# A decoder trunk's first norm with tokens on the partitions, and a first span of one row

## The chip, the cores and the metric

The kernel runs on one core of a Trainium2 chip. The metric is the time of one launch in device microseconds, lower is better. The profile was taken on one such execution.

## What is computed

Two decoder layers on 256 tokens of width 2048, all in float32: the first mixes tokens by retention with 8 heads, the second by a short gated convolution; each is followed by a SwiGLU block. Each of the four sub-layers begins with a norm whose scale and shift come from the conditioning vector c:

```
c_act = silu(c)
for i in range(DEPTH):
    mod = (c_act @ w_mod[i] + b_mod[i])[:, None, :]
    sh1, sc1, g1, sh2, sc2, g2 = split(mod, 6)
    h = rms_norm(x, norm1_g[i]) * (1 + sc1) + sh1
    x = x + g1 * mixer(h)          # layer 0: retention, layer 1: short convolution
    h = rms_norm(x, norm2_g[i]) * (1 + sc2) + sh2
    x = x + g2 * swiglu(h, ffn_w_in[i], ffn_w_out[i])
return rms_norm(x, final_g)
```

The retention starts with `h @ w_in`, which gives queries, keys, values and gates of all heads. Everything that the change touches lies before or in this product.

## The kernel before

**Layout.** Activations lie with the features on the partitions: 16 rows of 128 features by 256 tokens (`x[k]`, four tiles `x4`). A row of the normed activations, `h[k]`, is kept as a high part (float32r) and the remainder. Weights come as a stream of 1 MB chunks of 128 x 2048 (`w_all`), laid out on the host in the order of use. `prepare` takes half a chunk: ScalarE casts it to the high part (`hi`, L311), VectorE subtracts to get the low part (`lo`, L314). Each product is three passes on TensorE: high by high, high by low, low by high. There are four buffers for `hi` and four for `lo`, three for chunks. `take` keeps two halves ahead of TensorE after the first span.

**The modulation** is a product with a vector. It is not done on TensorE: each tile of `w_mod` (1 MB, features of one row by 2048) is multiplied by the spread `silu(c)` (`cb`) and summed by one instruction of VectorE (`reduced`, L657). Row k of the first norm needs two such tiles, `SC1` and `SH1`. `column` makes the two columns of the row on ScalarE (L666), `row` applies them (u at L682, h's high part at L685 on ScalarE, its low part at L686 on VectorE). `loaded` fetches the tiles into four buffers; `ahead_of(k)` fetches those of row k.

**Spans.** `ret_in` can't begin with all rows, as they are made one after the other. So the first product is cut into spans: a span is two heads' queries, keys and gates, over some rows, in eight banks of PSUM. `SPANS` lists them: heads 0, 1 over rows 0 and 1; heads 2, 3 over rows 0 to 5; heads 0, 1 over rows 2 to 9; heads 2, 3 over rows 6 to 11; head 4 over all 16 rows, four banks. For one row of two heads TensorE takes one chunk. After a span, `held` puts its banks away: the first time by a copy on ScalarE (L644), later by an add on VectorE (L641). The first four adds come at once, the next four are put into the list `due`.

**Order.** TensorE's order is that of the program. In this start VectorE's and ScalarE's order is written out by hand too (`manual_schedule`). In the first span each row's reductions stand between its two heads (`both_reduced`). In the spans behind it, `due` holds pairs of a step and something to do (make row k, reduce a tile for the next row, put a bank away), and `more`, which is called at each half step, does what is due. A step is one row of two heads.

**The first norm.** x is loaded in four pieces, ScalarE squares it, VectorE adds the squares, four small matmuls with ones sum over the partitions (`norm_sums`, L434), ScalarE makes the mean, GpSimd takes the root (L760), four matmuls spread it over the partitions (`norm_spread`, L455), ScalarE copies it out. VectorE then multiplies two rows of x by it at a time (`norm_two`, L674). Meanwhile TensorE spreads c over the partitions (L725), and ScalarE applies silu to it (L729).

All loads are issued by SyncE's queue in the order of the program; an issue waits there until its buffer is free.

Of the kernel before, what the change touches and what calls it, by code (L numbers as in the profile page):

```python
# [10 lines left out]
F32 = mybir.dt.float32  # L11
# [6 lines left out]
P = 128  # L18
# [169 lines left out]
def trunk(ctx: ExitStack, tc: tile.TileContext, x_in, c_in, pos_in, w_mod, cols_in, gain_in, tab_in, w_all, out):  # L188
# [46 lines left out]
    def mod_raw(t, pool=wpool, bufs=RAW_BUFS):  # L235
        raw = pool.tile([P, CHUNK], F32, tag="raw", name=name("raw"), bufs=bufs)
        nc.sync.dma_start(raw, w_mod[t])
        return raw
# [51 lines left out]
    def fetch():  # L290
        raw = wpool.tile([P, CHUNK], F32, tag="raw", name=name("raw"), bufs=RAW_BUFS)
        nc.sync.dma_start(raw, w_all[n_fetched[0]])
        n_fetched[0] += 1
        fetched.append(raw)
# [39 lines left out]
    def bank():  # L334
        return ps.tile([P, 2, S], F32, tag="bank", name=name("bank"))
# [245 lines left out]
    with ExitStack() as inner:  # L581
# [64 lines left out]
        with tc.tile_pool(name="start", bufs=1) as sp:  # L646
            raws_of, totals = {}, {}

            def loaded(which, k):
                if k < KT:  # L650
                    raws_of[which, k] = mod_raw(which * KT + k, sp, START_RAWS)

            def reduced(which, k):
                if k < KT:
                    raw = raws_of.pop((which, k))
                    total = totals[which, k] = tmp("msum", (P, 1), bufs=4)
                    nc.vector.scalar_tensor_tensor(raw, raw, 1.0, cb, op0=ALU.mult, op1=ALU.mult, accum_out=total)  # L657
# [11 lines left out]
            normed_x = {}  # L669

            def norm_two(i):
                t = normed_x[i] = rm.tile([P, 2, S], F32, tag=f"mid{18 + i % 2}", name=name("two"))
                both = x4[i // 2][:, 2 * (i % 2) : 2 * (i % 2) + 2, :]
                nc.vector.tensor_tensor(t, both, rb.unsqueeze(1).to_broadcast([P, 2, S]), op=ALU.mult)  # L674

            def row(k):

                a, b = (column(SC1, k), column(SH1, k)) if k else first_cols
                t = normed_x[k // 2][:, k % 2, :]
                full = tmp("u", bufs=3)  # L680
                if k:
                    nc.scalar.activation(full, t, AF.Identity, bias=b, scale=a)  # L682
                else:
                    nc.vector.tensor_scalar(full, t, a, b, op0=ALU.mult, op1=ALU.add)
                nc.scalar.activation(h[k][:, 0, :], t, AF.Identity, bias=b, scale=a)  # L685
                return lambda: nc.vector.tensor_tensor(  # L686
                    h[k][:, 1, :], full, h[k][:, 0, :].bitcast(F32), op=ALU.subtract
                )
# [6 lines left out]
            def after_scale(k):  # L695
                reduced(SH1, k + 1)
                if k % 2 == 0 and k + 2 < KT:
                    norm_two(k // 2 + 1)

            def ahead_of(k):  # L700
                loaded(SC1, k)
                loaded(SH1, k)
                if k < FIRST_KS + 2:
                    fetch()

            with tc.manual_schedule(engines={mybir.EngineType.DVE, mybir.EngineType.Activation}):
                c_row = sp.tile([1, D], F32, tag="raw", name=name("raw"), bufs=START_RAWS)
                nc.sync.dma_start(c_row, c_in)
                for i in range(4):
                    nc.sync.dma_start(x4[i], x_in[:, 4 * i : 4 * i + 4, :])  # L710
                loaded(SC1, 0)
                nc.sync.dma_start(cols, cols_in)
                loaded(SH1, 0)
                nc.sync.dma_start(tab, tab_in[:, : 1 + P])
                fetch()
# [3 lines left out]
                nc.vector.memset(eps, EPS)  # L719
                ahead_of(1)  # L720
# [10 lines left out]
                def square(i):  # L731

                    sq = [rm.tile([P, 2, S], F32, tag=f"mid{2 * i + n}", name=name("sq")) for n in range(2)]
                    for n in range(2):
                        nc.scalar.activation(sq[n], x4[i][:, 2 * n : 2 * n + 2, :], AF.Square)
                    return sq

                def added(a, b):
                    for n in range(2):
                        nc.vector.tensor_tensor(a[n], a[n], b[n], op=ALU.add)  # L740

                acc = square(0)
                for i in range(1, 4):
                    added(acc, square(i))
                for i in range(4):
                    silu(i)
                nc.vector.tensor_tensor(acc[0], acc[0], acc[1], op=ALU.add)
                nc.vector.tensor_tensor(acc[0][:, 0, :], acc[0][:, 0, :], acc[0][:, 1, :], op=ALU.add)
                pt = norm_sums([acc[0][:, 0, :]])
                reduced(SC1, 0)  # L750
                gain_1 = const.tile([P, KT], F32, tag="gain1", name="gain1")
                nc.vector.scalar_tensor_tensor(
                    gain_1, b_mod[:, SC1 * KT : (SC1 + 1) * KT], 1.0, gain[0][0], op0=ALU.add, op1=ALU.mult
                )
                reduced(SH1, 0)
                mean = tmp("rs", (P, 2), bufs=4)
                nc.scalar.activation(mean, pt[:, 0, 0:2], AF.Identity, bias=eps, scale=1.0 / D)
                first_cols = [column(SC1, 0)]
                r = tmp("rs", (P, 2), bufs=4)
                nc.gpsimd.tensor_tensor(r, mean, half, op=ALU.pow)  # L760
                rb = tmp("rb", bufs=1)
                nc.scalar.copy(rb, norm_spread(r))
                norm_two(0)
# [16 lines left out]
            at = 0.0  # L780
            for k in range(FIRST_KS, KT):
                steps = ROW_STEPS[k >= SPANS[1][1][1]]
                due.append((at, lambda k=k: (row(k)(), ahead_of(k + 2))))
                due.append((at + steps / 3, lambda k=k: reduced(SC1, k + 1)))
                due.append((at + steps * 2 / 3, lambda k=k: after_scale(k)))
                at += steps
            for i, turn in enumerate(angles()):
                due.append((at + (i + 1) * 0.5, turn))
# [13 lines left out]
            with tc.manual_schedule(engines={mybir.EngineType.DVE, mybir.EngineType.Activation}):  # L802
# [10 lines left out]
                while due:  # L813
                    due.pop(0)[1]()

# [341 lines left out]
```

## Time and profile before

| | |
|---|---|
| median of 3 runs | 2620.13 us (2616.75 to 2620.81) |
| the profiled execution | 2621.43 us, its span 2619.7 us |
| TensorE busy | 2587.4 us, 99% of the span |
| VectorE busy | 1982.7 us, 76% |
| ScalarE busy | 1248.5 us, 48% |
| moved by DMA | 689.62 MB, mean 263 GB/s |

The span counts from the first to the last instruction of the profiled execution; the device time includes what lies around it. In the profile's views PE is TensorE's matmuls, PEld its weight loads, DVE is VectorE, ACT ScalarE, POOL GpSimd, SPq SyncE's queue of DMA issues. A row of the timeline gives start and length in us, engine, line, operation, what is written and read, the number of merged instructions, and in brackets how long the engine had been idle and what released it.

### The profile page before, as it was taken

The numbers are of one execution on the slowest core, as the hardware profiler recorded it, in microseconds if no ns is written. First come the engines' busy times: TensorE is split into PE (matmuls) and PEld (weight loads), VectorE is DVE, ScalarE is ACT, GpSimd is POOL, SyncE is SP. The second block draws the span as 40 slices with busy tenths as digits, with TensorE's granted clock in tenths as the row PEclk, the third lists the DMA queues.
The fourth block names the chain that finished last, engine by engine and source line by source line (L and its number), as shares of the span: only waits on it lengthen the run. The fifth ranks groups of instructions, "written<-read, shape, count | busy, mean of one in ns | idle before, by whom it ended". The sixth has DMA issues, their size and how long they took to land.

```text
span 2619.7 us, 37456 instructions
## 1 busy us (share of the span) xinstructions
PE 2587.4 (99%) x14867; PEld 2283.7 (87%) x14867; DVE 1982.7 (76%) x2490; ACT 1248.5 (48%) x1784; POOL 148.4 (6%) x232
## 2 busy tenths in 40 slices
PE   7999999999999999999999999999999999999998
PEld 6898889888899888888888898888998888888887
DVE  7988977887698887777777889888887765555554
ACT  5544543444456444344444454444564443444443
POOL 0000000110000001101100001100000000000000
PEclk9999999999999999999999999999999999999999
DMA  9976668877686887777777758777777775555554
GB/s 398 393 288 224 252 243 305 291 253 277 243 303 244 314 298 275 286 282 283 283 277 273 282 216 326 293 267 265 265 268 261 263 251 193 193 187 186 191 193 145
DMA packets 96834, 689.62 MB, mean 263 GB/s; under 512 B 10753, under 2 KB 12177, under 8 KB 13713
## 3 DMA queue, kind: packets, MB, share of 16 engines
q1 hardware_dynamic: 96658, 687.23, 71.1%
q8 instruction: 116, 1.90, 0.3%
q14 instruction: 60, 0.49, 0.0%
HBM read 685.08 MB, written 2.11 MB: 262 GB/s over the span
## 4 chain that ended last, share of the span: by engine, by line
PE 87%; DMA 6%; DVE 5%; issue 1%; ACT 1%; ACTq 0%; POOLq 0%; POOL 0%; DVEq 0%
PE bank L356 37%; PE bank L359 19%; PE bank L372 7%; PE bank L371 7%; PE bank L373 7%; DMA raw<-w_all 4%; DVE lo L314 2%; PE bank L398 2%; PE bank L397 2%; PE bank L396 2%; DMA raw<-w_mod 2%; PE bank L529 1%; PE bank L531 1%; PE bank L530 1%; DVE raw L657 1%
## 5 line engine op out<-in xcount | busy, mean ns | idle before, releaser
L314 DVE TENSOR_TENSOR lo<-raw,hi 128x1024 fp32r<-128x1024 f32 x912 | 1113.0, 1224 | 562.3 <-ACT hi L311 560.5
L311 ACT CAST hi<-raw 128x1024 fp32r<-128x1024 f32 x912 | 953.6, 1050 | 1084.1 <-PE bank L356 478.9
L356 PE MATMUL bank<-h,hi 128*128 128x512 f32 x3296 | 1144.2, 390 | 0.2 <-ACT hi L311 0.2
L359 PE MATMUL bank<-h,lo 128*128 128x256 f32 x3296 | 929.6, 282 | 1.3 <-DVE lo L314 1.3
L356 PEld LDWEIGHTS bank<-h,hi 128*128 128x128 f32 x3296 | 618.6, 188 | 129.7 <-ACT hi L311 0.5
L359 PEld LDWEIGHTS bank<-h,lo 128*128 128x128 f32 x3296 | 622.9, 189 | 2.0 <-DVE lo L314 1.9
L245 DVE SCALAR_TENSOR_TENSOR raw<-raw,cb 128x2048 f32<-128x2048 f32 x160 | 365.8, 2286 | 24.6 <-DMA raw<-w_mod 24.2
L356 PE MATMUL bank<-mid,hi 128*128 128x512 f32 x922 | 319.8, 390 | 0.0
L359 PE MATMUL bank<-mid,lo 128*128 128x256 f32 x922 | 260.1, 282 | 1.4 <-DVE lo L314 1.4
L356 PEld LDWEIGHTS bank<-mid,hi 128*128 128x128 f32 x922 | 173.1, 188 | 36.2
L371 PE MATMUL bank<-hi,h 128*128 128x512 f32 x512 | 201.4, 393 | 2.0 <-DVE rm L641 1.4
L372 PE MATMUL bank<-lo,h 128*128 128x512 f32 x512 | 200.1, 391 | 0.8 <-DVE lo L314 0.8
L373 PE MATMUL bank<-hi,h 128*128 128x512 f32 x512 | 199.4, 389 | 0.0
L359 PEld LDWEIGHTS bank<-mid,lo 128*128 128x128 f32 x922 | 174.3, 189 | 1.7 <-DVE lo L314 1.7
L356 PE MATMUL bank<-rm,hi 128*128 128x512 f32 x496 | 172.5, 390 | 0.0
L398 PE MATMUL bank<-h,lo 128*128 128x256 f32 x512 | 146.2, 285 | 5.4 <-DVE lo L314 5.4
L396 PE MATMUL bank<-h,hi 128*128 128x256 f32 x512 | 145.6, 284 | 3.3 <-ACT h L685 3.3
L397 PE MATMUL bank<-h,hi 128*128 128x256 f32 x512 | 145.5, 284 | 0.7 <-DVE h L686 0.7
L359 PE MATMUL bank<-rm,lo 128*128 128x256 f32 x496 | 139.8, 282 | 0.0
L371 PE MATMUL bank<-hi,mid 128*128 128x512 f32 x352 | 137.0, 389 | 0.0
L372 PE MATMUL bank<-lo,mid 128*128 128x512 f32 x352 | 136.9, 389 | 0.0
L373 PE MATMUL bank<-hi,mid 128*128 128x512 f32 x352 | 136.9, 389 | 0.0
(175 smaller groups left out, 2700.0 us busy)
## 6 DMA issues: line engine op xcount, KB each, us to landing
raw<-w_all SPq DMA_DIRECT2D x456, 1024.0 KB, 4.8
raw<-w_mod SPq DMA_DIRECT2D x192, 1024.0 KB, 5.1
x<-x_in SPq DMA_DIRECT2D x4, 512.0 KB, 5.5
out<-xt SPq DMA_DIRECT2D x4, 512.0 KB, 3.0
decay<-tab_in SPq DMA_DIRECT2D x8, 128.0 KB, 2.4
x<-gain_in SPq DMA_DIRECT2D x2, 512.0 KB, 6.8
x<-gate_row SPq DMA_DIRECT2D x2, 512.0 KB, 5.3
cols<-cols_in SPq DMA_DIRECT2D x1, 152.0 KB, 8.6
```

What stands on the lines that cost most here:

```text
L245: nc.vector.scalar_tensor_tensor(raw, raw, 1.0, cb, op0=ALU.mult, op1=ALU.mult, accum_out=total)
L311: nc.scalar.copy(hi, raw)
L314: nc.vector.tensor_tensor(lo, raw, hi.bitcast(F32), op=ALU.subtract)
L356: nc.tensor.matmul(pt, hi, h, start=fresh and k == g.ks[0], stop=False, skip_group_check=True)
L359: nc.tensor.matmul(pt[:, 1, :], lo, h[:, 0, :], start=False, stop=last and k == g.ks[-1], skip_group_check=True)
L371: nc.tensor.matmul(o, ht[:, 0, :], hi, start=first, stop=False)
L372: nc.tensor.matmul(o, ht[:, 0, :], lo, start=False, stop=False)
L373: nc.tensor.matmul(o, ht[:, 1, :], hi, start=False, stop=last)
L396: nc.tensor.matmul(pt, hi, h[:, 0, :], start=first, stop=False, skip_group_check=True)
L397: nc.tensor.matmul(pt, hi, h[:, 1, :], start=False, stop=False, skip_group_check=True)
L398: nc.tensor.matmul(pt, lo, h[:, 0, :], start=False, stop=last, skip_group_check=True)
L529: nc.tensor.matmul(pt, hi, high, start=k == 0, stop=False, skip_group_check=True)
```

## The change

Nothing is changed behind the spans. In the start:

- x comes a second way, `xt_in`: tokens on the partitions, two halves of 128 tokens by 2048, in eight pieces of 128 x 512. The sums of squares run along the free dimension, half of the pieces on ScalarE and half on VectorE, each in one instruction with its sum.
- The roots are put on a diagonal (ScalarE scales the identity by them), and 32 matmuls turn x to the layout with features on the partitions and multiply it by the roots at once. ScalarE copies the eight banks into `x4` (`kept`), three of them before row 0 and five behind it. `x4` holds the normed x during the spans; the plain x is loaded into it after the last span.
- The first span has one row instead of two, and there are six spans in place of five. The reductions of row 1 come behind the first span and behind the preparation of chunk 1.
- The steps at which rows, loads and reductions are due are set anew, and the angles of the rotary embedding come later.
- The first loads are cut in two parts, and so are the first two reductions.

```diff
-SPANS = (((0, 1), (0, 2)), ((2, 3), (0, 6)), ((0, 1), (2, 10)), ((2, 3), (6, 12)), ((4,), (0, 16)))
+SPANS = (
+    ((0, 1), (0, 1)), ((2, 3), (0, 2)), ((0, 1), (1, 6)), ((2, 3), (2, 10)), ((0, 1), (6, 12)), ((4,), (0, 16)),
+)
-ROW_STEPS = (1.4, 2.0)
-START_RAWS = 4
+ROWS_AT, ROW_STEPS = (0.0, 2.4, 3.6, 4.8, 5.9), 2.0
+LOADS_AT, ANGLE_STEPS = (0.4, 1.9, 2.9), 6
+START_RAWS, KEPT_FIRST = 4, 3
...
             def row(k):
...
-                t = normed_x[k // 2][:, k % 2, :]
+                t = x[k]
...
             def both_reduced(k):
                 reduced(SC1, k + 1)
-                after_scale(k)
+                reduced(SH1, k + 1)
                 ahead_of(k + 2)
...
-                for i in range(4):
-                    nc.sync.dma_start(x4[i], x_in[:, 4 * i : 4 * i + 4, :])
-                loaded(SC1, 0)
+                for t, i in pieces:
+                    xt[t, i] = rm.tile([P, DV], F32, tag=f"mid{4 * t + i}", name=name("xt"))
+                    nc.sync.dma_start(xt[t, i], xt_in[t, :, i * DV : (i + 1) * DV])
+                nc.sync.dma_start(tab, tab_in[:, : 1 + P])
+                loaded(SC1, 0, 2)
                 nc.sync.dma_start(cols, cols_in)
-                loaded(SH1, 0)
-                nc.sync.dma_start(tab, tab_in[:, : 1 + P])
-                fetch()
+                loaded(SH1, 0, 2)
+                fetch(2)
...
+                warm = tmp("rs", (P, 2), bufs=4)
+                nc.gpsimd.tensor_tensor(warm, ones[:, 0:2], half, op=ALU.pow)
+                fetch()
                 ahead_of(1)
...
+                def squares_of(t, i):
+                    v, total = xt[t, i], part[:, i, t : t + 1]
+                    if i % 2:
+                        nc.vector.scalar_tensor_tensor(
+                            left[1], v, 1.0, v, op0=ALU.mult, op1=ALU.mult, accum_out=total
+                        )
+                    else:
+                        nc.scalar.activation(left[0], v, AF.Square, accum_out=total)
+                for t, i in pieces:
+                    squares_of(t, i)
+                    if i % 2:
+                        silu(2 * t + i // 2)
...
+                for t in range(2):
+                    nc.scalar.activation(roots[:, t, :], ident, AF.Identity, scale=r[:, t : t + 1])
+                for i in range(KT // 2):
+                    pt = bank()
                     for n in range(2):
+                        for t in range(2):
+                            j, c = divmod(2 * i + n, 4)
+                            v = xt[t, j][:, c * P : (c + 1) * P]
+                            nc.tensor.matmul(
+                                pt[:, n, t * P : (t + 1) * P], v, roots[:, t, :], start=True, stop=True
+                            )
+                    turned.append(pt)
+                def kept(i):
+                    nc.scalar.copy(x4[i // 2][:, 2 * (i % 2) : 2 * (i % 2) + 2, :], turned[i])
...
                     low[0]()
-                pts = packed(RET_SPANS[0], h, before=before, between=both_reduced, banks=banks)
+                    for i in range(KEPT_FIRST, KT // 2) if not k else ():
+                        kept(i)
+                pts = packed(RET_SPANS[0], h, before=before, banks=banks)
                 prepare()
                 prepare()
+                both_reduced(0)
...
+            for i, at in enumerate(rows_made):
+                k = FIRST_KS + i
+                due.append((at, lambda k=k: row(k)()))
+                due.append((LOADS_AT[i] if i < len(LOADS_AT) else at, lambda k=k: ahead_of(k + 2)))
+                if i:
+                    gap = min((at - rows_made[i - 1]) / 3, 0.5)
+                    due.append((at - 2 * gap, lambda k=k: reduced(SC1, k)))
+                    due.append((at - gap, lambda k=k: reduced(SH1, k)))
...
+        for i in range(4):
+            nc.sync.dma_start(x4[i], x_in[:, 4 * i : 4 * i + 4, :])
```

More of the change, by code (lines that the diff above doesn't have):

```diff
@@ L742, in trunk @@
[L742 to L750, printed above, removed]
+                part = rm.tile([P, 4, 2], F32, tag="mid8", name=name("part"))
@@ new lines, in trunk @@
+                for t, i in pieces:
+                    squares_of(t, i)
+                    if i % 2:
+                        silu(2 * t + i // 2)
+                both = tmp("rs", (P, 2), bufs=4)
+                nc.vector.tensor_tensor(part[:, 0:2, :], part[:, 0:2, :], part[:, 2:4, :], op=ALU.add)
+                nc.vector.tensor_tensor(both, part[:, 0, :], part[:, 1, :], op=ALU.add)
+                mean = tmp("rs", (P, 2), bufs=4)
+                nc.scalar.activation(mean, both, AF.Identity, bias=eps, scale=1.0 / D)
@@ L754, in trunk @@
                 )
-                reduced(SH1, 0)
-                mean = tmp("rs", (P, 2), bufs=4)
-                nc.scalar.activation(mean, pt[:, 0, 0:2], AF.Identity, bias=eps, scale=1.0 / D)
+                reduced(SH1, 0, 2)
+                kept(0)
                 first_cols = [column(SC1, 0)]
[L759 to L763, printed above, removed]
+                for i in range(1, KEPT_FIRST):
+                    kept(i)
                 first_cols.append(column(SH1, 0))
@@ L779, in trunk @@
             due, step = [], [0.0]
[L780 to L788, printed above, removed]
+            rows_made = list(ROWS_AT)
+            while len(rows_made) < KT - FIRST_KS:
+                rows_made.append(rows_made[-1] + ROW_STEPS)
+            for i, at in enumerate(rows_made):
[6 more added lines that the diff above has]
+                    due.append((at - gap, lambda k=k: reduced(SH1, k)))
+            due.sort(key=lambda d: d[0])
+            at = rows_made[-1] + ROW_STEPS
+            turns = []
+            due.append((rows_made[-4], lambda: turns.extend(angles())))
+            for i in range(ANGLE_STEPS):
+                due.append((at + (i + 1) * 0.5, lambda i=i: turns[i]()))
+            due.sort(key=lambda d: d[0])
             def more(n):
@@ L1150 @@
             tc,
-            *[aps[k] for k in ("x_in", "c_in", "pos_in", "w_mod", "cols_in", "gain_in", "tab_in", "w_all")],
+            *[aps[k] for k in ("x_in", "xt_in", "c_in", "pos_in", "w_mod", "cols_in", "gain_in", "tab_in", "w_all")],
             out,
```

59 lines of the change are left out of this document (31 added, 28 removed).

## The prediction

> **What bounds the kernel now.** The page first, then the busy time by stage.
>
> ```profile
> span 2619.7 us, 37456 instructions
> PE 2587.4 (99%) x14867; PEld 2283.7 (87%) x14867; DVE 1982.7 (76%) x2490; ACT 1248.5 (48%) x1784; POOL 148.4 (6%) x232
> 10.00:60.00 50.00, 37.92 (x217) 33.07 (x218) 43.01 (x47) 27.87 (x49) 1.39 (x1) 1.00 1.01 419
> 60.00:130.00 70.00, 66.69 (x418) 59.27 (x417) 67.59 (x70) 39.86 (x60) 0.00 (x0) 1.00 0.97 395
> 130.00:200.00 70.00, 70.00 (x448) 63.55 (x447) 59.78 (x71) 33.98 (x45) 0.00 (x0) 1.00 0.73 279
> ```
>
> The last three rows are stretches of the start (window, length, busy us of PE, PEld, DVE, ACT, POOL, clock, DMA share, GB/s). From 130 us on TensorE has no gap here; it misses 32.3 us in the whole span, 15.4 of them in the first two of these stretches, where the DMA engines are full (1.01) and VectorE is busy 67.6 of 70 us. The change only touches this start. Whatever it moves in the time at which TensorE has done the spans, it moves in the end. So I count not busy time but starts of TensorE's half steps (one row of one head, one half chunk of weights).
>
> ```profile
> 2.61 7.16 PE L725 MATMUL bank<-raw,ones 1*128 1x512 f32 x8 [2.61 <-DMA raw<-c_in]
> 15.47 1.22 PE L455 MATMUL bank<-tab,rs 128*128 128x128 f32 x4 [1.82 <-POOL rs L760]
> 19.18 0.58 PE L396 MATMUL bank<-h,hi 128*128 128x256 f32 x1 [2.48 <-ACT h L685]
> 22.57 0.41 PE L398 MATMUL bank<-h,lo 128*128 128x256 f32 x1
> 22.78 0.57 PE L371 MATMUL bank<-hi,h 128*128 128x512 f32 x1
> 68.38 0.39 PE L396 MATMUL bank<-h,hi 128*128 128x256 f32 x1 [0.84 <-ACT h L685]
> 71.80 0.28 PE L396 MATMUL bank<-h,hi 128*128 128x256 f32 x1
> 85.90 0.28 PE L396 MATMUL bank<-h,hi 128*128 128x256 f32 x1
> 89.77 0.28 PE L396 MATMUL bank<-h,hi 128*128 128x256 f32 x1
> 120.79 0.28 PE L396 MATMUL bank<-h,hi 128*128 128x256 f32 x1
> 122.22 0.40 PE L371 MATMUL bank<-hi,h 128*128 128x512 f32 x1
> 122.92 0.40 PE L371 MATMUL bank<-hi,h 128*128 128x512 f32 x1
> 123.61 0.28 PE L396 MATMUL bank<-h,hi 128*128 128x256 f32 x1
> 125.89 0.50 PE L371 MATMUL bank<-hi,h 128*128 128x512 f32 x1 [0.69 <-DVE rm L641]
> 127.62 0.50 PE L371 MATMUL bank<-hi,h 128*128 128x512 f32 x1 [0.76 <-DVE rm L641]
> 128.42 0.28 PE L396 MATMUL bank<-h,hi 128*128 128x256 f32 x1
> 1886.21 0.60 PE L455 MATMUL bank<-tab,rs 128*128 128x128 f32 x4
> ```
>
> An undisturbed half is 120.79 to 123.61, 2.82 us; a step of two heads is 5.64. The first starts at 19.18. Row 5 (eighth step) starts at 68.38: seven steps are 39.5, so 9.7 us are lost by then. After it, the halves from 68.38, 85.90 and 123.61 are late by 0.60, 1.05 and 1.99: 3.64. The last is a change of spans: the new span's eighth bank waits until VectorE has added the old one to what is held (L641).
>
> VectorE's queue, then ScalarE's with GpSimd's root:
>
> ```profile
> 55.36 2.29 DVE L657 SCALAR_TENSOR_TENSOR raw<-raw,cb 128x2048 f32<-128x2048 f32 x1
> 57.57 1.22 DVE L314 TENSOR_TENSOR lo<-raw,hi 128x1024 fp32r<-128x1024 f32 x1
> 59.15 0.43 DVE L686 TENSOR_TENSOR h<-u,h 128x256 fp32r<-128x256 f32 x1 [0.36 <-ACT h L685]
> 60.09 1.23 DVE L314 TENSOR_TENSOR lo<-raw,hi 128x1024 fp32r<-128x1024 f32 x1 [0.51 <-ACT hi L311]
> 61.23 2.28 DVE L657 SCALAR_TENSOR_TENSOR raw<-raw,cb 128x2048 f32<-128x2048 f32 x1
> 63.44 1.22 DVE L314 TENSOR_TENSOR lo<-raw,hi 128x1024 fp32r<-128x1024 f32 x1
> 117.88 2.47 DVE L641 TENSOR_TENSOR rm<-rm,bank 128x512 f32<-128x512 f32 x4
> 126.88 0.69 DVE L641 TENSOR_TENSOR rm<-rm,bank 128x512 f32<-128x512 f32 x1
> 10.49 2.04 ACT L729 ACTIVATE cb<-bank 128x512 f32<-128x512 f32 x4
> 13.69 0.26 ACT L757 ACTIVATE rs<-bank,eps 128x2 f32<-128x2 f32 x1 [1.15 <-PE bank L434]
> 16.73 0.37 ACT L762 COPY rb<-bank 128x256 f32<-128x256 f32 x1 [1.35 <-PE bank L455]
> 25.04 1.04 ACT L311 CAST hi<-raw 128x1024 fp32r<-128x1024 f32 x1 [4.98 <-DMA raw<-w_all]
> 35.84 3.98 ACT L644 COPY rm<-bank 128x512 f32<-128x512 f32 x8
> 40.58 2.00 ACT L311 CAST hi<-raw 128x1024 fp32r<-128x1024 f32 x2 [0.76 <-DMA raw<-w_all]
> 57.69 0.30 ACT L666 ACTIVATE s<-msum,cols 128x1 f32<-128x1 f32 x1 [2.96 <-DVE raw L657]
> 58.02 0.60 ACT L682 ACTIVATE u<-two,s,a 128x256 f32<-128x256 f32 x1
> 58.53 0.59 ACT L685 ACTIVATE h<-two,s,a 128x256 fp32r<-128x256 f32 x1
> 14.03 1.39 POOL L760 TENSOR_TENSOR rs<-rs,half 128x2 f32<-128x2 f32 x1 [13.60 <-ACT rs L757]
> ```
>
> Start to start: a reduction 2.21 (61.23 to 63.44), a lo 1.14 (60.09 to 61.23), a row's low half 0.34 of its 0.43, an add 0.60, a hi cast 0.95 to 1.0, a PSUM copy on ScalarE 0.50. A row needs its shift column after the reduction (55.36 to 57.69), then u and h: h is ready 3.8 us after the reduction started. If one lo lies between, VectorE idles 0.43 before the low half, if none, 1.6; after it, 0.6 until the next hi.
>
> Chunk 1 and chunk 3, with 8.2 and 14.2 MB queued up to their ends, were waited for until 25.04 and 40.58: 2.59 us per MB. I use this as the landing clock; the change keeps the queue full.
>
> **The change, part by part.**
>
> *Start.* The squares leave the chain (two adds of small tiles remain), and so do 4+4 small matmuls. c's spread still ends at 2.61+7.16 = 9.8; the last silu (2.04/4), the mean 0.26, the root 1.39 and one diagonal (at most the 0.37 of L762) give 12.4. New: 32 f32 matmuls with 128 columns, two instructions each like L455's, 64 in all, ahead of row 0 in TensorE's queue. Slow, L455's four start (1.22-0.58)/3 = 0.21 apart; fast, (0.60-0.27)/3 = 0.11. Bounds: 7.0 to 13.7 us. From 19.18 the array turned fast at 22.78, after 3.6 us. So 17 slow ones, then 47 × 0.11: they end at 21.2. The first matmul of row 0 comes 2 us later than the 19.18 of before, but fast. [...]
>
> *Copies.* ScalarE's copies of the turned banks are 0.50 each, eight, in place of eight squares. Three precede row 0: the third bank is turned at about 17.1 (24 instructions), copy and shift column end at 17.9, chunk 0's first half (4.7 MB) has landed at 16.0, its hi and h[0] are ready at 19.5, its lo and the low half at 20.5, hidden since TensorE turns until 21.2. Five stand ahead of hi 0b: the last waits for the end of the turning, 21.5, so hi 0b starts at 22.0 and VectorE's lo 0b at 23.1. VectorE idles for it; row 1's reductions, which could run there, now stand behind the lo of chunk 1.
>
> *VectorE from 23.1 to row 5*, in the order that `due` gives (0b is chunk 0, second half; S and H the scale's and shift's reductions):
> 0b 1a 1b S1 H1 = 7.8, to 30.9 (S1 and H1 have landed at 22.4 and 25.0); idle 1.6, row 1, idle 0.6: 33.4. 2a 2b 3a S2 3b H2 4a = 10.1: 43.6; 0.43, row 2, 0.6: 45.0. 4b S3 5a H3 5b = 7.8: 52.8; 0.43, row 3: 53.6. S4 6a H4 6b = 6.7: 60.3; 0.43, row 4: 61.1. Chunk 7 has 22.2 MB up to its end: 61.3, its hi a cast later, so 7a starts at 62.4 (chunk 5, at 45.8, and chunk 6, at 53.5, are in time). 7a S5 7b H5 = 6.7: 69.1; 1.6: row 5 at 70.7.
> TensorE meets row 1 at step 2 about 2 us late, rows 3, 4 and 5 again late; row 5 starts at 70.7 against 68.38: **+2.3**. The half products (norm_two, 0.6 for two rows) are gone, but H5 now directly precedes row 5, and chunk 7 lands no earlier. A start up to 0.7 earlier is eaten by chunk 7.
>
> *Changes of spans.* Two in place of one put eight banks against VectorE's adds (the two first ones go to ScalarE's copies, 35.84, in time; the last needs four banks). In before, adds from 117.88 to 127.57 made the bank, wanted at 120.79+2.82+1.43+0.70 = 125.7, 1.9 late. By the new `due` S6 lies behind the fourth add and H6 before the seventh. From row 5: low half and 8a 8b to 73.9, four adds 76.3, S6 2.2, add, 9a, add, H6, add, 9b, add: 85.4. Wanted: step end 76.5 + 4.95 = 81.45; **3.95** late. At the next change VectorE has slack, but its adds can start only after lo 16b, whose buffer TensorE frees one step before the end E: lo done at E-3.4, four adds E-1.0, then the same 9.1 and a 0.1 to TensorE: E+8.2 against E+4.95: **3.25**.
>
> *Hidden.* The second load of x, 2 MB at about 195 us, meets a share of 0.73 and no waiting copy (5 us at the landing clock if it had to be waited for whole). The angles' later place puts some 6 us of VectorE behind the last span's weights, two prepared halves (5.6) cover it: 0 to 2. GpSimd's warm-up root lies ahead of xt: 0. xt's eight loads move the same 2 MB.
>
> Sum: 2.3 + 3.95 + 3.25 - 3.64 (the losses that followed in before) = **+5.9**. The profiled execution took 2621.43 (its span and 1.7 around it), 1.3 above the median of 2620.13; on the median: 2626.0.
>
> **The rivals.**
>
> *The turning stays slow.* [...] 64 × 0.21 ends at 26.1 and lo 0b starts at 28.0, 4.9 later; chunk 7's wait of 1.3 is swallowed, so row 5 is 3.6 later: +9.5, 2629.6. Chance 0.18. [...]
>
> *VectorE gets ahead* (faster). One mechanism: the reductions of rows 1 to 5 are done while TensorE still multiplies reused rows, so that each h is ready when it is wanted. Then only the start (21.2 for 19.18), row 1's 2 us and two changes of spans at the old 1.99 remain: 21.2 + 2 + 4 = 27.2, against 19.18 + 9.7 + 3.64 = 32.5 now: -5.3, 2614.8. It decides if row 5 starts by 64. For it: the landing clock allows it up to chunk 7 (61.3 and two casts). Against it: 15 lo, 10 reductions and 5 low halves are 41 us of VectorE's work from 23.1 on, and TensorE needs 39.5 us for its seven steps from 21.2 on. Chance 0.14.
>
> **How the numbers follow.** The forecast has 0.68. Its own range is +2.5 to +9: row 5 within 2 us (chunk 7 and the idle bubbles), each change of spans within 1, the angles 0 to 2. 0.2%, 5.2 us, is about what a measurement of this kernel can tell from no change; 55 in 100 of the forecast's range lie above it. Slower: 0.18 + 0.37 = 0.55; within: 0.31; faster: 0.14. The 8 in 10 reach from 2614 to 2633; what is left out is the better half of the faster rival and the far end of the slow turning.
>
> **What would show it.** Right: 64 matmuls on the diagonal from about 12.4 to 21, lo 0b near 23, no idle VectorE over 1.7 us from there to row 5, TensorE waiting for h at rows 3 to 5, row 5 at 70 to 72, and two waits for L641's adds of 3 to 4 us. Wrong: row 5 before 66, or changes of spans without a wait; then the sum turns.

## The result and the profile after

| | before | after |
|---|---|---|
| median of 7 runs each, taken together | 2617.21 us (2616.25 to 2620.81) | 2626.78 us (2624.60 to 2627.70) |
| ratio after to before | | 1.0032, 95% interval 1.0020 to 1.0044 |
| profiled execution, its span | 2621.43, 2619.7 | 2626.78, 2625.0 |

The change makes the kernel slower by 0.32%, some 8 us by the ratio, 9.6 by the medians. The absolute time lies 0.8 from the predicted one, but that flatters the forecast: it added 5.9 to a base of 2620.1, the median of three runs, and all seven taken together put the base at 2617.2. The difference is what has to be explained: 5.9 forecast, in a range of 2.5 to 9, and 8 to 10 found.

The page of after, its first lines, and the stretches of the start as in the prediction (window, length, busy us of PE, PEld, DVE, ACT, POOL, clock, DMA share, GB/s):

```profile
span 2625.0 us, 37613 instructions
PE 2596.1 (99%) x14923; PEld 2293.8 (87%) x14923; DVE 1983.3 (76%) x2498; ACT 1253.1 (48%) x1793; POOL 144.2 (5%) x233
10.00:60.00 50.00, 42.54 (x260) 38.56 (x261) 39.37 (x50) 34.76 (x60) 1.61 (x1) 0.97 1.01 409
60.00:130.00 70.00, 64.79 (x384) 57.39 (x384) 59.63 (x62) 31.32 (x45) 0.00 (x0) 0.95 0.94 361
130.00:200.00 70.00, 67.24 (x428) 60.49 (x427) 63.53 (x67) 34.37 (x48) 0.00 (x0) 1.00 0.87 313
```

PE is busier than before from 10 to 60 us, which says nothing good: the turning, 9.9 us of it, is new work. Between 60 and 200 PE now has 8.0 us without work, where before had 3.3; VectorE is not full in any of the three stretches; and the clock is under 1.00 in the first two, which no row quoted of before had shown. Where the time goes is seen in single rows, here of the timeline of after in the order of their starts (start, length, engine, line, ..., idle before and releaser):

```profile
10.81 0.69 DVE L746 SCALAR_TENSOR_TENSOR left<-xt 128x512 f32<-128x512 f32 x1 [0.62 <-DMA xt<-xt_in]
12.38 1.61 POOL L762 TENSOR_TENSOR rs<-rs,half 128x2 f32<-128x2 f32 x1 [9.26 <-ACT rs L760]
14.48 9.87 PE L774 MATMUL bank<-roots,xt 128*128 128x128 f32 x64 [4.77 <-DMA raw<-w_mod]
24.10 0.36 PE L404 MATMUL bank<-h,hi 128*128 128x256 f32 x1
25.95 1.22 DVE L322 TENSOR_TENSOR lo<-raw,hi 128x1024 fp32r<-128x1024 f32 x1 [2.73 <-ACT hi L319]
63.66 2.00 ACT L319 CAST hi<-raw 128x1024 fp32r<-128x1024 f32 x2 [0.18 <-DMA raw<-w_all]
73.03 0.38 PE L404 MATMUL bank<-h,hi 128*128 128x256 f32 x1 [3.26 <-ACT h L693]
86.13 0.50 PE L379 MATMUL bank<-hi,h 128*128 128x512 f32 x1 [1.06 <-DVE rm L649]
87.13 0.68 DVE L649 TENSOR_TENSOR rm<-rm,bank 128x512 f32<-128x512 f32 x1
87.86 0.76 PE L379 MATMUL bank<-hi,h 128*128 128x512 f32 x1 [0.77 <-DVE rm L649]
136.32 0.50 PE L379 MATMUL bank<-hi,h 128*128 128x512 f32 x1 [1.83 <-DVE rm L649]
138.05 0.50 PE L379 MATMUL bank<-hi,h 128*128 128x512 f32 x1 [0.77 <-DVE rm L649]
```

The last piece of xt is squared at 10.81, the turning starts at 14.48 and row 0's first matmul at 24.10 (19.18 in before). The row of 25.95 is the low part of chunk 0's second half. TensorE waits 3.26 for row 5 and then twice at each change of spans for VectorE's adds (L649). These are the waits that the prediction named; what it did not name is that matmuls get slower after some of them, and that chunk 7 (63.66) lands late and the low part of 25.95, forecast for 23.1, starts late.

To add this up I use one measure for all kernels: "late" is the start of a half step of TensorE less 2.82 us (unrounded 2.817) for each half step before it. It starts at the first matmul's time, and only losses raise it. Half 14 is row 5; half 59 is the last of the spans. All are read from the timelines:

| kernel | first matmul | row 5 starts | late at row 5 | late at half 59 | span |
|---|---|---|---|---|---|
| before | 19.18 | 68.38 | 28.9 | 32.7 | 2619.7 |
| before, a second profile | 19.21 | 68.44 | 29.0 | 32.8 | 2616.4 |
| after | 24.10 | 73.03 | 33.6 | 43.15 | 2625.0 |
| n_norm | 24.35 | 70.76 | 31.3 | 34.5 | 2618.2 |
| n_spans | 19.34 | 70.69 | 31.25 | 41.2 | 2623.7 |
| n_spans_x8 | 21.00 | 71.48 | 32.0 | 42.1 | 2623.2 |
| b_x8 | 20.26 | 70.26 | 30.8 | 34.7 | 2617.5 |
| a_warm | 21.61 | 71.51 | 32.1 | 42.2 | 2622.5 |
| a_adds | 24.05 | 73.36 | 33.9 | 38.1 | 2618.8 |
| a_last | 24.18 | 73.45 | 34.0 | 37.6 | 2618.5 |
| a_fill | 24.34 | 74.56 | 35.1 | 37.0 | 2618.1 |
| b_adds | 19.02 | 68.41 | 29.0 | 30.75 | 2614.7 |
| a_half | 23.98 | 70.24 | 30.8 | 34.55 | 2616.7 |
| a_halfload | 22.09 | 64.37 | 24.9 | 28.7 | 2609.9 |

From before to after the spans end 10.4 us later: 4.65 are there at row 5, and 5.8 come behind it.

### The profile page after: what moved, and what is told of

Read it like the earlier page. It is cut to its first block, busy times and chain, and to the rows that moved or that the text cites. A ratio compares the mean times of both kernels' runs of the same rounds, so it can differ in the third digit from the quotient of the medians.

```text
span 2625.0 us, 37613 instructions
## 1 busy us (share of the span) xinstructions
PE 2596.1 (99%) x14923; PEld 2293.8 (87%) x14923; DVE 1983.3 (76%) x2498; ACT 1253.1 (48%) x1793; POOL 144.2 (5%) x233
## 4 chain that ended last, share of the span: by engine, by line
PE 94%; DVE 3%; DMA 2%; issue 1%; ACT 1%; SPq 0%; ACTq 0%; POOLq 0%; POOL 0%; DVEq 0%
PE bank L364 39%; PE bank L367 21%; PE bank L379 7%; PE bank L380 7%; PE bank L381 7%; PE bank L406 2%; PE bank L405 2%; PE bank L404 2%; PE bank L537 1%; PE bank L539 1%; PE bank L538 1%; DMA raw<-w_all 1%; DVE lo L322 1%; DVE raw L667 1%; PE bank L927 1%
```

## The experiments

**1. Which half of the change costs the time?** n_norm has the new norm (x turned, loads in parts) with the old spans and order:

```diff
-    ((0, 1), (0, 1)), ((2, 3), (0, 2)), ((0, 1), (1, 6)), ((2, 3), (2, 10)), ((0, 1), (6, 12)), ((4,), (0, 16)),
+    ((0, 1), (0, 2)), ((2, 3), (0, 6)), ((0, 1), (2, 10)), ((2, 3), (6, 12)), ((4,), (0, 16)),
 ... (the old list of due steps, reductions between the heads of the first span)
```

> The new norm alone (tokens on the partitions, 32 turning matmuls, loads in two parts), with the five spans, the order and the due steps of before. Theory 1 (the order of VectorE's work costs, not the norm): lo of the first chunk's second half comes some 2 to 4 us later than the 25.47 of before, but VectorE's idle stretch of 4.3 us at 37 to 42 (it waits for chunk 3) swallows it: row 5 starts at 68 to 69.5, the spans end within 1.5 us of before, ratio 0.9995 to 1.001. Rival (the late first matmul, 24.1 for 19.2, carries through): row 5 at 72 to 73, ratio 1.0015 to 1.002.

n_spans has the old norm with the new spans, the new list of due steps and the new order of the loads:

```diff
 ... (norm, squares and loads of x as before)
-    ((0, 1), (0, 2)), ((2, 3), (0, 6)), ((0, 1), (2, 10)), ((2, 3), (6, 12)), ((4,), (0, 16)),
+    ((0, 1), (0, 1)), ((2, 3), (0, 2)), ((0, 1), (1, 6)), ((2, 3), (2, 10)), ((0, 1), (6, 12)), ((4,), (0, 16)),
```

> The six spans with their order and due steps alone, with the norm of before. Theory 1: row 5 at about 70.7, since chunk 7 lands at 61 to 62 whatever the start; two waits for VectorE's adds of 3 to 4 us at the changes of spans; the spans end 6 to 9 us later than before, ratio 1.002 to 1.0035. Rival (the norm is the cause): row 5 at 68 or earlier, ratio below 1.001.

Measured against before: n_norm 1.0009 (1.0000 to 1.0017), n_spans 1.0029 (1.0019 to 1.0039). At the end of the spans n_norm is 1.75 later than before, n_spans 8.4, the two together 10.15, against 10.4 for after: they add up. n_norm's row 5 (70.76) fell between the two theories, neither of which put it there. Some four fifths of the loss at the end of the spans belong to the spans and their order, the rest to the new norm, which is the turning of x and its loads together. At row 5 the two halves cost the same, 2.4 and 2.3.

**2. The changes of spans.** a_adds is after with all eight banks of a closed span added at once, with no reductions between the adds:

```diff
-                        if key not in ahead or i < 4:
+                        if key not in ahead or i < 8:
```

> The changed kernel with all eight adds of a change of spans at once, ahead of the reductions. Theory 1: both waits of TensorE for VectorE's adds (3.0 and 3.55 us) are gone and so is the slow clock at 87 to 91 us (0.9): the spans end 6.5 to 7.5 us earlier than in the changed kernel, ratio to before 1.0005 to 1.001. Rival (VectorE is behind in any case, so the reductions pushed back come late instead): TensorE waits for rows 6 to 9 by as much, ratio stays at 1.003.

The same edit on the kernel before is b_adds:

> The kernel before with all eight adds of a change of spans at once. Theory 1: its one wait at the change (1.99 us of delay) is gone, nothing else moves: -2 us, ratio 0.999 to 0.9995. Rival: the pushed-back reduction makes a later row late, ratio 1.000.

Rows of VectorE and TensorE, first of a_adds:

```profile
76.55 5.31 DVE L649 TENSOR_TENSOR rm<-rm,bank 128x512 f32<-128x512 f32 x8
159.01 4.86 DVE L649 TENSOR_TENSOR rm<-rm,bank 128x512 f32<-128x512 f32 x8
167.28 0.39 PE L406 MATMUL bank<-h,lo 128*128 128x256 f32 x1 [1.22 <-DVE lo L322]
```

The eight adds take 4.9 to 5.3 us in one go and no bank is waited for any more: from row 5 to half 59 a_adds loses 4.2 us where after loses 9.6. Two of the 4.2 are new: ahead of the last span the block of adds, followed by two reductions (from 163.79 and 167.14), now holds a low part up (1.22, with shorter waits on both sides); the other two are a slow clock, below. The ratio is 1.0011 (1.0002 to 1.0020). On the kernel before, the same edit takes 2 us off the end of the spans and gives 0.9990 (0.9981 to 0.9999): some 2.5 us faster than before, which is itself the faster of the two kernels, and only just clear of the noise.

a_last puts the last change of spans back as it was:

```diff
-                        if key not in ahead or i < 8:
+                        if key not in ahead or i < 4 or g is not RET_SPANS[-2]:
```

> The changed kernel with eight adds at once at the changes of spans, but the last change left as it was (there the next span needs four banks only). Theory 1: no wait for the adds, and the 2.0 us that TensorE lost near 171 us with all adds at once is gone: the spans end 9 us earlier than in the changed kernel (half 59 late by about 36.1 instead of 43.15), ratio 1.0005 to 1.0012. Rival: the loss near 171 us has another cause and stays (38.1).

It ends at 37.6, 0.5 better than a_adds and 1.5 short of the expectation: the low part is still waited for 1.14 at 170.09, with VectorE's reductions of 161.5 and 166.0 now between the adds instead of behind them. After, with that same order, does not wait there: its TensorE comes 7 us later there (late 43.1 at half 39 against 36.1, and still 43.1 at half 59). Part of what is won at the first two changes runs into VectorE's queue at the third, in either order of its work. Ratio 1.0004 (0.9995 to 1.0013).

**3. The slow matmuls.** In after the granted clock changes at 57.21, 60.62, 74.27, 77.69, 87.93 and 91.34, each a whole number of 3.41 us from the one before; the matmuls show it too, 0.12 us apart up to 57.22 and 0.21 behind it. Windows of after, cut at these moments and at others a whole number of 3.41 us away:

```profile
53.80:57.21 3.41, 1.79 (x10) 1.12 (x9) 3.06 (x5) 2.39 (x5) 0.00 (x0) 1.00 0.99 396
57.21:60.62 3.41, 3.41 (x13) 2.95 (x12) 3.41 (x4) 1.38 (x3) 0.00 (x0) 0.50 1.00 413
70.86:74.27 3.41, 1.16 (x7) 0.97 (x8) 1.41 (x4) 2.67 (x5) 0.00 (x0) 1.00 0.98 401
74.27:77.69 3.42, 3.42 (x13) 2.94 (x12) 3.42 (x5) 0.59 (x1) 0.00 (x0) 0.50 1.00 402
84.52:87.93 3.41, 1.58 (x9) 0.90 (x7) 3.41 (x6) 2.33 (x4) 0.00 (x0) 1.00 0.58 173
87.93:91.34 3.41, 3.41 (x13) 3.13 (x14) 2.09 (x3) 1.04 (x1) 0.00 (x0) 0.50 1.00 408
135.71:139.13 3.42, 2.04 (x9) 1.43 (x10) 3.42 (x5) 2.39 (x5) 0.00 (x0) 1.00 0.72 240
139.13:142.54 3.41, 3.41 (x26) 3.15 (x25) 2.74 (x3) 1.65 (x2) 0.00 (x0) 1.00 1.01 353
```

Three times a stretch in which TensorE is busy for 1.79 us or less is followed by one at half the clock (0.50; the half steps from 56.06 and 73.03 take 4.8 us instead of 2.82); the fourth pair shows a stretch with waits, 2.04 busy, that is not. a_fill is a_last with matmuls that keep the array streaming in the waits for rows 3 and 5. Their weights are zero and they add to a bank that is in use, so that the sums stay as they are:

```diff
+FILL = {3: 13, 5: 40}
 ...
+                def before(k):
+                    more(n)
+                    for _ in range(FILL.get(k, 0) if g is RET_SPANS[2] else 0):
+                        nc.tensor.matmul(pts[0][:, 0, :], zero, h[0][:, 0, :], start=False, stop=False, ...)
```

> The same, with matmuls of zero weights added to a bank (they change no sum) in the waits for row 3 (13) and row 5 (40). Theory 2 (an idle of about half of a 3.4 us window drops TensorE's clock to half for the next window, and the two slow halves cost 2.0 us each): no slow clock at 56 to 60 and 73 to 77 us; the first costs nothing, since row 5 comes from VectorE at 73 in any case, the second 2.0: spans end 2 us earlier than without the fillers, 34.1. Rival (zero weights don't count as activity, or the fillers make row 5 late): clock drops as before, no gain or a loss up to 1 us.

The timeline of a_fill, the two groups of fillers, and the same 30 us in it and then in a_last:

```profile
54.61 1.69 PE L846 MATMUL bank<-h,zero 128*128 128x256 f32 x13
69.87 4.86 PE L846 MATMUL bank<-h,zero 128*128 128x256 f32 x40
50.00:80.00 30.00, 28.60 (x190) 25.63 (x189) 26.50 (x29) 12.94 (x20) 0.00 (x0) 1.00 1.01 419
```

```profile
50.00:80.00 30.00, 24.66 (x132) 21.13 (x131) 26.12 (x29) 12.18 (x20) 0.00 (x0) 0.89 1.00 409
```

The clock stays at 1.00 where a_last has 0.89: with the waits filled, here by matmuls with zeros (28.60 us busy for 24.66), it is not lost. From row 5 to half 59 a_fill loses 1.9 where a_last loses 3.6: that is 1.7 of the 2.0 that the slow window costs. Forty fillers are too many, though: they run to 74.7 and row 5 starts 1.1 later, so the net gain is 0.6, not the 2 expected, and in the time nothing is left of it (1.0009, 1.0000 to 1.0017, where a_last has 1.0004).

**4. What sets row 5?** a_half leaves out half of the modulation's sum for rows 1 to 15 (each reduction runs over 1024 of 2048 columns). a_halfload leaves out the same half and doesn't load it either. Each edit beside after:

```diff
-                    n, some = CHUNK // parts, [...]
+                    n, some = (CHUNK // parts if not k else CHUNK // 2), [...]
```

> The changed kernel with the reductions of rows 1 to 15 over half of their columns (it leaves out the other half of the product with c for these rows; the loads stay). Theory 1 (VectorE's queue and, behind it, chunk 7's landing set row 5): each reduction takes 1.15 instead of 2.21, row 5 starts at 66 to 69 instead of 73.0, no earlier, since chunk 7 lands at 61 to 64 and lo, S, lo, H and the row follow. Rival (DMA alone sets row 5): 72 to 73. Rival (VectorE alone): 62 to 64.

```diff
+                    if k:
+                        raw = sp.tile([P, CHUNK], F32, tag="raw", name=name("raw"), bufs=START_RAWS)
+                        nc.sync.dma_start(raw[:, : CHUNK // 2], w_mod[which * KT + k][:, : CHUNK // 2])
```

> The same with the tiles of rows 1 to 15 also loaded to half only (5 MB less up to chunk 7, which then lands about 13 us earlier). Theory 1: both limits are gone, TensorE waits for no row of 2 to 5 by more than 1 us, row 5 at 64 to 65. Rival (a third limit, ScalarE or the buffers): later than 67.

Row 5 moved by 2.8 with half of the reductions, and by another 5.9 with half of the loads. In each timeline, chunk 7's high part (the first row) and row 5's first matmul (the second); n_spans, a_half and a_halfload in this order:

```profile
61.33 2.00 ACT L314 CAST hi<-raw 128x1024 fp32r<-128x1024 f32 x2 [1.34 <-DMA raw<-w_all]
70.69 0.58 PE L399 MATMUL bank<-h,hi 128*128 128x256 f32 x1 [4.41 <-ACT h L688]
```

```profile
63.00 2.00 ACT L319 CAST hi<-raw 128x1024 fp32r<-128x1024 f32 x2 [2.57 <-DMA raw<-w_all]
70.24 0.45 PE L404 MATMUL bank<-h,hi 128*128 128x256 f32 x1 [3.51 <-ACT h L693]
```

```profile
57.13 2.00 ACT L319 CAST hi<-raw 128x1024 fp32r<-128x1024 f32 x2 [2.20 <-DMA raw<-w_all]
64.37 0.57 PE L404 MATMUL bank<-h,hi 128*128 128x256 f32 x1 [2.47 <-ACT h L698]
```

From the one to the other it is 9.36 in n_spans and 9.37 in after (63.66 to 73.03), 7.24 in a_half and 7.24 in a_halfload: a fixed stretch of VectorE's queue behind a landing, 2.1 shorter where its two reductions are halved. a_half missed its expectation because of that landing: with half of the reductions the weights come only 0.7 sooner, and the cast waits 2.57 for them. a_halfload's row 5 is where its theory put it, but not for its reason: chunk 7 came 6.5 sooner instead of 13 and still holds row 5 up, for which TensorE waits 2.47 where no more than 1 was expected.

How much the landing holds back is seen in VectorE's wait ahead of chunk 7's low part, here in after and then in n_spans:

```profile
64.74 1.23 DVE L322 TENSOR_TENSOR lo<-raw,hi 128x1024 fp32r<-128x1024 f32 x1 [0.80 <-ACT hi L319]
```

```profile
62.41 1.23 DVE L317 TENSOR_TENSOR lo<-raw,hi 128x1024 fp32r<-128x1024 f32 x1 [1.96 <-ACT hi L314]
```

In a_half this wait is 3.20. Behind rows 1 and 2 of after, where no landing is waited for, it is 0.51 and 0.52. So chunk 7 sets row 5 in n_spans and a_half, but in after only some 0.3 us hang on it: VectorE's own queue, which begins late there (25.95), would by itself put row 5 at about 72.7, an estimate from these waits. The two limits nearly meet.

So the question is why VectorE's queue begins late in after, and why chunk 7 lands at 61.3 in n_spans and at 63.7 in after. Two runs ask it. a_warm lets the turning start with a released clock:

```diff
+                for _ in range(WARM):                                  # WARM = 10
+                    nc.tensor.matmul(idle[:, 0:P], ones, ones, start=True, stop=True)
                 turned = []
```

> The kernel after, with ten matmuls of ones on ones (128 x 512, float32) ahead of the turning, while x is still being loaded, so that the turning finds the clock released. Theory: the turning's 9.9 us shrinks to 7 to 7.5 and the first token matmul starts at 21.3 to 22.2 instead of 24.1; but row 5 stands on VectorE's queue and the landings of the weights, so it starts at 71.5 to 73.0 instead of 73.0, and the end of the spans moves by less than 1.5. Rival: the start is a chain that carries everything behind it along: then row 5 starts at 70.5 to 71.2 and the end of the spans comes 2 to 2.8 earlier.

(The ten have 128 columns, not 512 as the expectation says.) n_spans_x8 is n_spans with x loaded in pieces as small as those of xt; b_x8 is the same edit on the kernel before:

```diff
-                for i in range(4):
-                    nc.sync.dma_start(x4[i], x_in[:, 4 * i : 4 * i + 4, :])
+                for i in range(8):
+                    nc.sync.dma_start(x4[i // 2][:, 2 * (i % 2) : 2 * (i % 2) + 2, :], x_in[:, 2 * i : 2 * i + 2, :])
```

> n_spans (norm of before, spans and order of after), with x loaded in eight loads of 256 KB with 2 KB rows, as xt is, in place of four of 512 KB. In n_spans, a_warm and after, row 5 starts 9.36, 9.37 and 9.37 us after chunk 7's hi cast could start (61.33, 62.14, 63.66), so with the new spans row 5 hangs on chunk 7's landing. Theory: the small loads leave the load queue thinner from 4 to 8 us (after: 272 and 230 GB/s, n_spans: 369 and 354), some 0.5 MB that every later load is behind: chunk 7's hi starts at 62.2 to 63.0 and row 5 at 71.6 to 72.4, against 61.33 and 70.69 in n_spans. Rival: the size of the loads costs nothing, and after is behind for its later chain (diagonal, turning) alone: chunk 7's hi at 61.2 to 61.5, row 5 at 70.6 to 70.9.

> The kernel before, with x loaded in eight loads of 256 KB in place of four of 512 KB. Theory: the first matmul starts within 0.6 of 19.2 to the late side (the last piece of x lands later), and the load queue is 0.4 to 0.6 MB behind at 10 us; row 5 starts at 69 to 70 against 68.4, as part of the 2.4 us by which n_norm (new norm, old spans) was late there. Rival: with the old spans VectorE's queue sets row 5, the landings have slack: row 5 at 68.3 to 68.8, and n_norm's 2.4 come from its later first matmul.

The timelines of a_warm and n_spans_x8:

```profile
9.70 4.27 PE L770 MATMUL bank<-ones 128*128 128x128 f32 x20
14.38 7.48 PE L778 MATMUL bank<-roots,xt 128*128 128x128 f32 x64 [0.41 <-ACT roots L766]
62.14 2.00 ACT L320 CAST hi<-raw 128x1024 fp32r<-128x1024 f32 x2 [1.15 <-DMA raw<-w_all]
71.51 0.58 PE L405 MATMUL bank<-h,hi 128*128 128x256 f32 x1 [4.23 <-ACT h L694]
```

```profile
62.12 1.99 ACT L314 CAST hi<-raw 128x1024 fp32r<-128x1024 f32 x2 [1.52 <-DMA raw<-w_all]
71.48 0.58 PE L399 MATMUL bank<-h,hi 128*128 128x256 f32 x1 [4.58 <-ACT h L688]
```

and what the DMA engines moved in short windows, for after, n_spans, n_spans_x8 and a_warm in this order; the last two columns are the share and GB/s:

```profile
4.00:6.00 2.00, 2.00 (x3) 0.66 (x2) 0.35 (x1) 1.21 (x3) 0.00 (x0) 1.00 0.84 272
6.00:8.00 2.00, 2.00 (x4) 0.85 (x3) 0.95 (x3) 1.21 (x3) 0.00 (x0) 1.00 0.77 230
28.00:32.00 4.00, 4.00 (x27) 3.65 (x26) 4.00 (x5) 4.00 (x9) 0.00 (x0) 1.00 0.92 334
```

```profile
4.00:6.00 2.00, 2.00 (x3) 0.66 (x2) 0.00 (x0) 0.55 (x2) 0.00 (x0) 1.00 0.98 369
6.00:8.00 2.00, 2.00 (x4) 0.95 (x3) 0.64 (x2) 1.75 (x4) 0.00 (x0) 1.00 0.99 354
```

```profile
4.00:6.00 2.00, 2.00 (x3) 0.66 (x2) 0.00 (x0) 1.22 (x2) 0.00 (x0) 1.00 0.91 309
6.00:8.00 2.00, 2.00 (x4) 0.77 (x3) 0.13 (x1) 0.71 (x2) 0.00 (x0) 1.00 1.01 318
```

```profile
28.00:32.00 4.00, 4.00 (x29) 3.70 (x28) 3.37 (x4) 2.14 (x6) 0.00 (x0) 1.00 1.01 422
```

Small loads alone move chunk 7 from 61.33 to 62.12 and row 5 from 70.69 to 71.48 (each 0.1 short of the range expected, and far outside the rival's). The released clock alone moves chunk 7 from 63.66 to 62.14 and row 5 from 73.03 to 71.51: the load queue's dip at 28 to 32 us (334 GB/s) is gone with it (422). Both stay 9.36 and 9.37 apart. So of the 2.33 us, 0.8 go with the eight small loads and 1.5 with the slow turning. With the turning VectorE's low part of chunk 0's second half moves, from 25.95 in after to 23.46 in a_warm, and with that the buffers come free for which the loads behind wait: the load queue's longest wait for a low part, up to 66 us, is 8.1 us in after and 5.8 in a_warm. This split is one of several: with the turning left late, an earlier chunk 7 could gain after no more than the 0.3 above. Nor does the small loads' part come by the load queue alone, as in n_spans_x8 the first matmul too starts 1.66 later than in n_spans.

a_warm's end of the spans is 0.95 earlier than after's, as its theory had it, with row 5 at the edge of the range. The end is in part luck: up to half 33 a_warm is 3.1 earlier (late 36.5 against 39.5), as it has no slow clock at the first change; at the second it loses 5.7 where after loses 3.55, with the clock at half from 132.91 to 139.74.

b_x8 missed its expectation to the late side: first matmul 20.26, row 5 70.26, end of the spans 34.7; the last two are 1.9 and 2.0 later than before. In the old order, too, the pieces cost nearly what the whole new norm costs there (n_norm 2.4 at row 5, 1.75 at the end). Whether it is the 2 KB rows, the number of loads, or both, these runs don't tell apart.

**5. Why do the two profiles differ by 5.3 us only?** before_again is the kernel before, profiled a second time.

> The kernel before, unchanged, profiled a second time. Theory: the profiles of before and after differ by only 5.3 us although the half steps of TensorE are 10.4 us apart at the end of the spans, because the profiled execution of before has single waits late in the kernel (0.51 at 229, 0.51 and 0.76 at 469 to 471, 0.20 and 0.76 at 894 to 896, 0.53 at 902, 1.41 at 1815.8) that belong to that execution and not to the kernel: then row 5 starts at 68.4 again, the last half step of the spans stands 32.7 behind an even beat again, most of those late waits are gone, and the span is 2615 to 2617. Rival: the late waits belong to the kernel and new work in after takes them away: then they come back at the same places and the span is 2619 to 2620.

Single waits of TensorE late in the first profile of before, then in the second:

```profile
469.24 0.50 PE L371 MATMUL bank<-hi,h 128*128 128x512 f32 x1 [0.51 <-ACT hi L311]
895.51 0.38 PE L359 MATMUL bank<-h,lo 128*128 128x256 f32 x1 [0.76 <-DVE lo L314]
1815.78 0.39 PE L359 MATMUL bank<-mid,lo 128*128 128x256 f32 x1 [1.41 <-DVE lo L314]
```

```profile
1812.56 0.38 PE L359 MATMUL bank<-mid,lo 128*128 128x256 f32 x1 [1.12 <-DVE lo L314]
```

The start is the same within 0.1 us, the waits at 469 and 895 are gone, the one at 1815 is not, and the span is 2616.4. Against this profile after is 10.3 us later at the end of the spans, 9.3 at 789 us and 8.6 at the end: most of what is lost in the start arrives, and about 1.7 is given back on the way. It fits the medians (9.6) and the ratio (5 to 11.5 us).

## Why the prediction was right, and where its steps failed

The direction and, in the main, the mechanism held: VectorE's queue and chunk 7 set row 5, and two changes of spans wait for adds. Of the sum (+5.9 at the end of the spans, +10.4 measured) three terms were as forecast and two were too small. Three of the signs that the prediction had named were missed: the turning ran from 14.48 to 24.10, not from 12.4 to 21, the low part of chunk 0's second half came at 25.95, not near 23, and row 5 at 73.03, not at 70 to 72.

- *Start.* Turning forecast from 12.4 to 21.2, measured 14.48 to 24.10. The last piece of xt was waited for until 10.81, where the forecast let the squares end under c's spread at 9.8; the root took 1.61 for 1.39, the two diagonals 0.69 for 0.37. The turning itself took 9.6 against 8.8: the clock was released at 19.7, 5.2 us after its start (the turning's instructions start 0.21 apart up to there, 0.11 behind), not 3.6. The 3.6 was read one row too early, too: in before the matmul of 22.78 is still a slow one (0.57, and the next starts 0.41 later); the first fast one starts at 23.19, 4.0 after 19.18. The clock was released, so the rival of a slow turning fell, and a_warm shows how much it was worth (7.2 us with the clock at full). The forecast took the delay for a fixed one; it was 4.0 us in before and 5.2 in after, and what sets it these traces don't show.
- *Row 5: +2.3 forecast, +4.65 measured.* The order of VectorE's queue was right to the instruction, and so was its length: from the low part of chunk 0's second half to row 5 the forecast has 47.6 (23.1 to 70.7) and the trace 47.1 (25.95 to 73.03), and most of the 0.5 between them is the wait at chunk 7, 1.3 forecast and 0.9 found. What failed is where the queue begins. It began 2.85 late, as the turning ended 2.9 late, and only 0.5 of that was swallowed at chunk 7: this is the 2.35. "A start up to 0.7 earlier is eaten by chunk 7" took chunk 7 for a fixed floor, and "the change keeps the queue full", with "xt's eight loads move the same 2 MB", costed the loads at nothing. But chunk 7's load waits for buffers that VectorE frees, and the eight loads are slower: chunk 7 came at 63.66, not 61.3, so that it swallowed little, and a_warm's start, 2.5 us earlier, moved row 5 by 1.5. That n_spans has the forecast 61.3 and 70.7 to the digit (61.33 and 70.69) is in part luck: it has the old norm, whose start the forecast was not made for.
- *First change of spans: 3.95 forecast.* From row 5's start to the end of the last add the forecast has 14.7, and the trace 87.13 + 0.60 - 73.03 = 14.7; the bank's wait is 87.86 - 73.03 - 10.75 = 4.1. But the spans lose 5.9 there, 1.8 of it from matmuls at half the clock from 87.93 to 91.34, which the forecast did not have. The slow windows behind rows 3 and 5 cost after nothing of their own, as TensorE had to wait for VectorE behind them anyway; a_adds and a_last, without that wait, pay the 2.0.
- *Second change: 3.25 forecast, 3.55 measured* (half 33 to half 34, 6.37 for 2.82). *What before lost later: 3.64 forecast, 3.79 measured.* *Angles, second load of x, GpSimd's warm-up root: nothing*, and nothing found (0.1 remains of the sum).
- The sum of the misses: 2.35 at row 5, 1.9 at the first change (nearly all of it clock), 0.3 at the second and 0.1 left over, less 0.15: 4.5 of 10.4 - 5.9.
- *On the base.* The forecast stands on the median of three runs, 2620.13; with four more runs it is 2617.21, 2.9 lower. Two errors of opposite sign, a base too high and a difference too small, met near the measured time: that it came within 0.8 us is luck.
- *VectorE gets ahead*, the rival on the faster side, needed row 5 by 64. Only a_halfload comes near (64.37), with half of the modulation's loads left out.

## What to carry to other kernels

When a start is bound by a full load queue, count each edit there in megabytes of delay, pieces and buffer releases included: smaller loads of the same bytes, and a late consumer that holds a buffer, moved chunk 7 by 0.8 and 1.5 us here. Before splitting a loop to feed an engine earlier, price the boundary that the split adds, and see whether what stands between the pieces of work at that boundary can stand behind them (here one number, four adds at once or eight, gave back 5 of the 10.4 us that the change had lost at the end of the spans). Take two profiles of the kernel before when the question is under 0.3%: single late waits come and go from one execution to the next.

## What was not expected of the hardware

- *A wait of 1.54 us was followed by half the clock.* A single wait (after, 54.52 to 56.06) came ahead of 3.4 us at half the clock (57.21 to 60.62). What this goes with in these traces is TensorE's busy time in each 3.41 us between the moments at which the clock can be seen to change. Of such windows at full clock, from the release to 205 us in eleven of the traces, 15 with 1.80 us busy or less had half the clock behind them, and none with 1.90 or more; one with 1.58 kept it (before, 23.16 to 26.57, right behind the release), and why is open. The way back is not the same: a_warm lost the clock behind 1.76 and, still slow, did not regain it behind 2.98, while after did behind 3.41 (57.21 to 60.62). The two windows of a_warm:

```profile
129.50:132.91 3.41, 1.76 (x13) 1.35 (x11) 3.41 (x5) 0.27 (x1) 0.00 (x0) 1.00 0.73 279
132.91:136.32 3.41, 2.98 (x6) 1.98 (x7) 3.41 (x5) 2.06 (x4) 0.00 (x0) 0.50 0.79 252
```

  Where a_fill filled the waits with matmuls (50 to 80 us, 28.60 busy for a_last's 24.66) the clock was 1.00 for 0.89.
- *2 MB in eight loads of 2 KB rows were slower than in four of 4 KB rows*: 309 and 318 GB/s against 369 and 354 (n_spans_x8 and n_spans, 4 to 8 us). Row 5 came 0.8 us later with them. The traces do not tell the length of the rows from the number of loads.
- *7 us of matmuls over one partition left the array slow.* c's spread takes 7.16 us, its starts 0.87 apart. In a_warm the ten matmuls of ones over 128 partitions begin directly behind it, at 9.70, and their 20 instructions took 4.27 us, 0.21 each; the 64 of the turning, behind them, took 7.48, 0.12 each. After's turning, behind the same spread and without the ten, took 9.87. The clock column of the windows reads 1.00 in after's start too (4 to 8 us); there it is the spacing of the matmuls that shows the slow array.
